# A log-sum-exp without its maximum: range checks and a branch to a safe loop

## The chip, the cores and the metric

The kernel runs on one core of a Trainium2 chip. The metric is the time of one execution on the device, in microseconds (us). The engines are written as the profile writes them: PE is TensorE (PEld its weight loads), DVE is VectorE, ACT is ScalarE, POOL is GpSimd, and SP is SyncE, which here issues nearly all transfers.

## The reference

```
x (8, 2048, 2048) float32, bias (8, 256) float32
B, S, D = x.shape; H = 8; Dh = 256
x_heads = x.reshape(B, S, H, Dh).transpose(0, 2, 1, 3) + bias[None, :, None, :]
x_tiled = np.repeat(x_heads, 2, axis=2)
mx  = x_tiled.max(axis=-1, keepdims=True)
lse = mx.squeeze(-1) + np.log(np.exp(x_tiled - mx).sum(axis=-1))
```

Both inputs are drawn from a standard normal distribution. For each of 8 x 2048 rows and each of 8 heads, one number comes out: the logarithm of the sum of 256 exponentials of x plus bias. Each is written twice, so the output is (8, 8, 4096). The input has 134 MB, the output 1 MB.

## The kernel before

**It takes no maximum.** It sums the exponentials of x + bias as they are and takes the logarithm of the sum. Where a value lies far from zero, such a sum would overflow or vanish; the reference, which subtracts the maximum first, would not.

**Tiles.** The work is cut into 64 tiles of 2 rows on each of 128 partitions (K = 2, 2 MB each), eight tiles to a batch. Eight tiles fit on chip (the buffers xb). SP issues the loads, two tiles at a time up to tile 41 (L158), then one tile or less at a time (L170). A load into a buffer waits for the last reader of the tile that was there eight tiles earlier.

**The work of a bulk tile** (tiles 0 to 53, mode BULK) is split by heads:

- Heads 0 to 2: PE puts the bias into PSUM (L267) and adds x by a product with the identity (L326). ACT takes the exponential. For head 0 it sums on the way (L337, with an accumulator), for heads 1 and 2 it writes the exponentials back (L344).
- Head 3: ACT takes the exponential of x alone (L382), and DVE multiplies it by exp(bias), which lies in PSUM (w_ps, L394).
- Heads 4 to 7: POOL adds the bias in place (L376, a tensor of 128x2048 elements), then ACT takes the exponential (the same L382).
- DVE sums heads 1 to 7 in one reduction (L401, 128x3584).

The sums of batch b go into a tile R[b] of 128 x 128 numbers, those of the last batch into R_last.

**The end of the input** (tiles 54 to 63) runs in other modes, row by row, so that less is left to do when the last bytes land. There DVE multiplies by exp(bias) and sums in one instruction (L417), and POOL folds the last head or two (L433, L441), whose 32 remaining columns DVE sums (L447). ACT's part for PE's heads is L357.

**The output.** Two tiles after a batch has ended, finish(b) transposes its sums on PE (L461) and ACT writes their logarithm, each twice, to res (L471). With the seventh batch done, SP stores seven batches at once (store, L475). For the last batch finish_last does the same at the end: transpose (L482), logarithm (L488), store (L489).

**Order.** The whole kernel stands in a manual schedule: each engine issues its instructions in the order in which the program names them, and semaphores order the engines among each other. After the manual schedule has ended, the closing instructions of the program stand on L623, the line of the surrounding context: the wait for outstanding transfers, a drain of each engine and synchronising events on all of them. Instructions that load the bias and build its factors (L199 to L228) stand before the first tile.

Of the kernel before, what the change touches and what calls it, by code (L numbers as in the profile page):

```python
# [8 lines left out]

F32 = mybir.dt.float32  # L10
BF16 = mybir.dt.bfloat16
ACT = mybir.ActivationFunctionType
ALU = mybir.AluOpType

# [22 lines left out]
SINGLE_F1 = dict(pe=1, acc=1, g0=8, late=False, fold=1)  # L37
TRIPLE = dict(pe=3, acc=3, g0=8, late=False, fold=0)
FOLD = 32

STAGES = [
    (0, (BULK,)),
# [13 lines left out]
def kernel(  # L56
# [6 lines left out]
    nc = tc.nc  # L63
    P = nc.NUM_PARTITIONS
    B, S, D = x.shape
    H, Dh = bias.shape
# [13 lines left out]
    sb = ctx.enter_context(tc.tile_pool(name="sb", bufs=1))  # L80
# [4 lines left out]
    brow = sb.tile([1, D], F32, name="brow")  # L85
    b_rep = sb.tile([P, D - G0], F32, name="b_rep")
    w_sb = sb.tile([P, D - W1], F32, name="w_sb")
    ident = sb.tile([P, P], F32, name="ident")
    ones = sb.tile([1, P], F32, name="ones")
    ones3 = sb.tile([3, P], BF16, name="ones3")  # L90
    b3 = sb.tile([3, CPE], BF16, name="b3")
    bparts = sb.tile([1, 3, CPE], BF16, name="bparts")
    brest = sb.tile([1, 2, CPE], F32, name="brest")

    R = [sb.tile([P, KB, H, NB], F32, name=f"R{b}") for b in range(B - 1)]
    R_last = sb.tile([P, H, NBLK, K], F32, name="R_last")
    res = sb.tile([H * NB, B - 1, P, KB, 2], F32, name="res")
    res_last = sb.tile([P, P, 2], F32, name="res_last")
    xbs = [sb.tile([P, KB, D], F32, name=f"xb{i}") for i in range(NBUF // TB)]
    xts = [xb[:, k : k + K] for xb in xbs for k in range(0, KB, K)]  # L100
    w_ps = pp.tile([P, W2 - W0], F32, name="w_ps")
# [7 lines left out]
    def modes_of(t):  # L109
        return [modes for t0, modes in STAGES if t0 <= t][-1]  # L110

    def pieces(t):

        if len(modes_of(t)) == 1:
            return [(0, K, 0, D)]
        cols = [[(0, D)]] * K if t < T - 1 else LAST_COLS
        return [(k, k + 1, c0, c1) for k in range(K) for c0, c1 in cols[k]]
# [72 lines left out]
    for set_idx, (_name, funcs) in enumerate(get_activation_tables(nc.m.arch).items()):  # L190
        if ACT.Exp in funcs and ACT.Ln in funcs:
            nc.scalar.add_instruction(
                mybir.InstLoadActFuncSet(
                    name=nc.get_next_instruction_name(),
# [23 lines left out]
    def spread(dst, c0, c1):  # L218
        nc.tensor.matmul(  # L219
            dst, lhsT=ones, rhs=brow[:, c0:c1], start=True, stop=True  # L220
        )
# [4 lines left out]
    w_late = w_ps[:, 0 : G0 - W0]  # L226
    spread(w_late, W0, G0)
    nc.scalar.activation(out=w_late, in_=w_late, func=ACT.Exp)  # L228

    def first_factors():  # L230
        spread(one_ps, V0, W0)
        nc.scalar.activation(out=one_ps, in_=one_ps, func=ACT.Exp)

    def other_factors():
        nc.scalar.activation(
            out=w_ps[:, G0 - W0 :], in_=b_rep[:, 0 : W2 - G0], func=ACT.Exp
        )
        nc.scalar.activation(out=w_sb, in_=b_rep[:, W1 - G0 :], func=ACT.Exp)

# [55 lines left out]
    def add_x(m, t, k0, c0, c1, got):  # L295


        heads = []
        for ka, kb, c, w, bank, p in got:
            if not c0 <= c < c1:  # L300
                continue
            mm = nc.tensor.matmul(  # L302
                p,
                lhsT=ident,
                rhs=xts[t % NBUF][:, ka:kb, c : c + w],
                start=False,
                stop=True,
            )
            on_bank(bank, on_x(t, mm, [loads[t, k0, c0]]))
            for i in range(0, (kb - ka) * w, Dh):  # L310
                k, cw = divmod(i, w)
                heads.append((ka + k, (c + cw) // Dh, bank, p[:, i : i + Dh], mm))
        return heads

    def keep_warm():
        for _ in range(NWARM):
            nc.tensor.matmul(  # L317
                tp[:, 0], lhsT=ident, rhs=ident, start=True, stop=True
            )

    def late_heads(m, t, got, sums):
# [13 lines left out]
        def pe_part():  # L335
            for k in range(K):
                act = nc.scalar.activation(  # L337
                    out=xts[t % NBUF][:, k, 0:Dh],
                    in_=got[0][:, k * Dh : (k + 1) * Dh],
                    func=ACT.Exp,  # L340
                    accum_out=sums[:, k, 0:1],
# [87 lines left out]
    def fold(t, k, h0, h1, sums, after):  # L429
# [8 lines left out]
        n = Dh  # L438
        while n > FOLD:
            n //= 2  # L440
# [5 lines left out]
        def add_up():  # L446
            red = nc.vector.tensor_reduce(  # L447
                out=sums[:, k, h0:h1],
                in_=v[:, :, 0:FOLD],
                op=ALU.add,  # L450
# [6 lines left out]
    def finish(b):  # L457

        nr = H * NB
        for k in range(KB):  # L460
            nc.tensor.transpose(  # L461
                out=tp[0:nr, k],
                in_=R[b][:, k].rearrange("p h n -> p (h n)"),
                identity=ident,
            )
        tv = bass.AP(
            tensor=tp.tensor,
            offset=tp.offset,
            ap=[[tp.ap[0][0], nr], [1, P], [P, KB], [0, 2]],
        )  # L470
        nc.scalar.activation(out=res[:, b], in_=tv, func=ACT.Ln)  # L471

    def store():
# [3 lines left out]
            in_=res.rearrange("q b p k r -> q b (p k r)"),  # L477
        )

    def finish_last():  # L480
        last = tp[:, KB - 1]
        nc.tensor.transpose(  # L482
            out=last, in_=R_last.rearrange("p h n k -> p (h n k)"), identity=ident
        )
        tv = bass.AP(
            tensor=last.tensor, offset=last.offset, ap=[last.ap[0], [1, P], [0, 2]]
        )
        nc.scalar.activation(out=res_last, in_=tv, func=ACT.Ln)  # L488
        nc.sync.dma_start(  # L489
            out=out[B - 1].rearrange("h (n r) -> (h n) r", r=2 * P),  # L490
            in_=res_last.rearrange("q p r -> q (p r)"),
        )


    def sums_of(t):

        b, blk = divmod(t, NBLK)
        if b < B - 1:
            return R[b][:, blk % TB * K :, :, blk // TB]
        return R_last[:, :, blk, :].rearrange("p h k -> p k h")  # L500
# [20 lines left out]
    for t in range(T):  # L521
        if t == T_FACTORS:
            other_factors()
        xt = xts[t % NBUF]
        sums = sums_of(t)
        for k0, k1, c0, c1 in pieces(t):
            m = modes_of(t)[k0]
            add = None
            heads = []
            if c0 == 0:  # L530
                bias_here = bias_there
            if m["late"]:
                pe_part = late_heads(m, t, bias_here, sums)
            else:
                heads = add_x(m, t, k0, c0, c1, bias_here)

                def pe_part(t=t, heads=heads, sums=sums):
                    for k, h, bank, p, mm in heads:
                        sum_biased(t, k, h, bank, p, mm, sums)

            if c0 == 0:
                if next_units and not m["late"]:
                    bias_there = put_bias(*next_units.pop(0))
                if t > T_PROMPT and m["g0"] == H:
                    keep_warm()
                if m["g0"] < H:
                    add = g_add(m, t, k0, k1)
                if t < T - 1 or k0 == 0:
                    flush(for_pool)
            if t == T_PROMPT and (k0, c0) == (0, 0):  # L550
                first_factors()
            h0 = max(c0 // Dh, m["pe"])
            h1 = min(c1 // Dh, m["g0"])
            hf = max(h0, min(h1, H - m["fold"]))
            if h0 < h1 and not m["late"]:
                done = exp_inplace(
                    t, xt[:, k0:k1, h0 * Dh : h1 * Dh], loads[t, k0, c0]
                )
                if hf < h1:
                    for_pool.append(fold(t, k0, hf, h1, sums, done))  # L560
            if c0 == 0:
                flush(for_pe)
            if not m["late"]:
                for k in range(k0, k1):
                    for h in range(h0, hf):
                        weigh(
                            t,
                            xt[:, k, h * Dh : (h + 1) * Dh],
                            h,
                            sums[:, k, h : h + 1],  # L570
                            done,
                        )

            def pool_part(t=t, m=m, k0=k0, k1=k1, sums=sums, add=add):
                if add:
                    later(m, t, k0, k1, sums, add)
                if k1 == K:
                    reload(t)

            for_pool.append(pool_part)  # L580
            if m["g0"] < H:
                pe_part()
                if m["late"]:
                    bias_there = put_bias(*next_units.pop(0))
            elif heads:
                for_pe.append(pe_part)

        fb, at = divmod(t - 2, NBLK)
        if fb >= 0 and at == NBLK - 1:
            finish(fb)  # L590
            if fb == B - 2:
                store()
    flush(for_pe)
    flush(for_pool)
    finish_last()

    order.__exit__(None, None, None)


# [28 lines left out]
```

## Time and profile before

| | |
|---|---|
| time, median of 3 runs (lowest to highest) | 325.45 us (325.33 to 326.03) |
| span of the profiled execution, first to last instruction | 323.1 us |
| median of the runs less that span | 2.35 us |
| mean granted TensorE clock | 0.913 |
| last x tile's reduction of the bulk (L401) begins | 276.12 us |
| last sum on DVE (L447) begins | 319.41 us |
| last store issued (L489), median time to landing | 320.52 us, 1.7 us |

The profile comes from one execution and carries no time of its own other than the span; the runs were timed apart from it. The page gives the busy time of each engine, then the span in 40 equal slices with the busy share in tenths, then the queues. The chain of work that ended last is followed back from the last instruction: at each step to whatever released it, or to the instruction before it on its engine. In a list of waits, the columns are the engine and line that waited, what released it, the total in us, the number of times and the longest. In a timeline a row has its start in us, its duration, engine, line, operation, and output and input with their shapes; in square brackets stands how long the engine was idle before, and what ended that. "L12" is line 12 of the kernel.

### The profile page before, as it was taken

The numbers are of one execution on the slowest core, as the hardware profiler recorded it, in microseconds if no ns is written. First come the engines' busy times: TensorE is split into PE (matmuls) and PEld (weight loads), VectorE is DVE, ScalarE is ACT, GpSimd is POOL, SyncE is SP. The second block draws the span as 40 slices with busy tenths as digits, with TensorE's granted clock in tenths as the row PEclk, the third lists the DMA queues.
The fourth block names the chain that finished last, engine by engine and source line by source line (L and its number), as shares of the span: only waits on it lengthen the run. The fifth ranks groups of instructions, "written<-read, shape, count | busy, mean of one in ns | idle before, by whom it ended". The sixth has DMA issues, their size and how long they took to land.

```text
span 323.1 us, 2398 instructions
## 1 busy us (share of the span) xinstructions
PE 270.3 (84%) x691; PEld 102.9 (32%) x691; DVE 283.9 (88%) x306; ACT 265.8 (82%) x426; POOL 287.7 (89%) x120
## 2 busy tenths in 40 slices
PE   5999999889978769977869886888997786599984
PEld 2333333333323223322323322333333232035442
DVE  1037779999999998999899899898999999999995
ACT  1148679889869976988888978889998998899995
POOL 6939998999999999999999999999999999858874
PEclk9979799979979996998997997997999999559998
DMA  8999999999999999999999999999999999999995
GB/s 311 457 402 454 450 400 439 450 402 446 438 414 446 432 418 443 430 422 447 422 426 441 422 434 442 404 426 430 432 422 431 430 428 425 416 422 421 419 401 170
DMA packets 8830, 135.42 MB, mean 419 GB/s; under 512 B 1041, under 2 KB 1425, under 8 KB 2417
## 3 DMA queue, kind: packets, MB, share of 16 engines
q1 hardware_dynamic: 8720, 135.27, 98.6%
q8 instruction: 5, 0.08, 0.1%
q14 instruction: 7, 0.06, 0.0%
q10 hardware_dynamic: 98, 0.01, 0.0%
HBM read 134.23 MB, written 1.05 MB: 419 GB/s over the span
## 4 chain that ended last, share of the span: by engine, by line
DMA 40%; POOL 18%; ACT 17%; PE 14%; DVE 9%; issue 0%; SPq 0%; DVEq 0%
DMA xb<-in_x_dram 40%; POOL xb L376 18%; ACT xb L382 11%; DVE R L401 6%; PE pair L326 5%; PE one_ps L326 3%; PE pair L267 3%; ACT xb L357 2%; PE one_ps L267 2%; DVE xb L417 2%; PE pair L219 1%; ACT xb L337 1%; DVE xb L394 1%; ACT res L471 1%; ACT xb L344 1%; DMA brow<-in_bias_dram 1%
## 5 line engine op out<-in xcount | busy, mean ns | idle before, releaser
L376 POOL TENSOR_TENSOR xb<-xb,b_rep 128x2048 f32<-128x2048 f32 x57 | 257.6, 4539 | 20.7 <-DMA xb<-in_x_dram 20.6
L401 DVE TENSOR_REDUCE R<-xb 128x14 f32<-128x3584 f32 (+1 forms) x56 | 214.5, 3830 | 1.9
L382 ACT ACTIVATE xb<-xb 128x2560 f32<-128x2560 f32 (+5 forms) x77 | 157.1, 2050 | 10.3 <-POOL xb L376 10.1
L326 PE MATMUL pair<-xb,ident 128*128 128x512 f32 x216 | 114.3, 656 | 0.0
L326 PE MATMUL one_ps<-xb,ident 128*128 128x512 f32 x108 | 67.5, 710 | 11.5 <-DMA xb<-in_x_dram 11.5
L344 ACT ACTIVATE xb<-pair 128x1024 f32<-128x1024 f32 x54 | 55.5, 1027 | 23.2 <-PE pair L326 23.0
L326 PEld LDWEIGHTS pair<-xb,ident 128*128 128x128 f32 x216 | 46.2, 214 | 61.3 <-issue 61.3
L394 DVE TENSOR_TENSOR xb<-xb,w_ps 128x512 f32<-128x512 f32 x54 | 36.7, 681 | 26.2 <-ACT xb L382 26.2
L337 ACT ACTIVATE xb<-one_ps 128x256 f32<-128x256 f32 x108 | 40.0, 380 | 6.6 <-PE one_ps L326 6.6
L267 PEld LDWEIGHTS <-ones 3*128 3x128 bf16 (+1 forms) x192 | 16.9, 95 | 80.8 <-issue 71.4
L267 PE MATMUL one_ps<-b,ones 3*128 3x512 bf16 x49 | 18.6, 380 | 25.4 <-ACT xb L337 25.3
L267 PE MATMUL pair<-b,ones 3*128 3x512 bf16 x98 | 29.0, 375 | 0.0
L326 PEld LDWEIGHTS one_ps<-xb,ident 128*128 128x128 f32 x108 | 17.2, 200 | 33.9 <-DMA xb<-in_x_dram 18.0
L302 PE MATMUL pair<-xb,ident 128*128 128x512 f32 (+1 forms) x36 | 21.7, 689 | 5.7 <-DMA xb<-in_x_dram 5.7
L417 DVE CUSTOM_DVE_ANT_0 xb<-xb,w_ps 128x256 f32<-128x256 f32 x61 | 22.4, 418 | 0.0
L337 ACT ACTIVATION_READ_ACCUMULATOR xb<-one_ps 128x1 f32 x108 | 22.3, 207 | 0.0
L441 POOL TENSOR_TENSOR xb<-xb 128x128 f32<-128x128 f32 (+3 forms) x39 | 13.8, 355 | 3.1
L433 POOL TENSOR_TENSOR xb<-xb,w_sb 128x256 f32<-128x256 f32 (+1 forms) x13 | 10.0, 771 | 5.2 <-ACT xb L382 4.5
L317 PE MATMUL tp<-ident 128*128 128x128 f32 x84 | 13.7, 302 | 0.0
L317 PEld LDWEIGHTS tp<-ident 128*128 128x128 f32 x84 | 11.1, 200 | 3.5 <-issue 3.0
L357 ACT ACTIVATE xb<-pair 128x256 f32<-128x256 f32 x33 | 11.9, 364 | 0.0
L417 DVE CUSTOM_DVE_ANT_0 xb<-xb,one_ps 128x256 f32<-128x256 f32 x27 | 10.6, 415 | 0.1
(42 smaller groups left out, 83.4 us busy)
## 6 DMA issues: line engine op xcount, KB each, us to landing
xb<-in_x_dram SPq DMA_DIRECT2D x20, 4096.0 KB, 21.5
xb<-in_x_dram SPq DMA_DIRECT2D x17, 2048.0 KB, 22.7
xb<-in_x_dram SPq DMA_DIRECT2D x12, 1024.0 KB, 22.7
xb<-in_x_dram SPq DMA_DIRECT2D x4, 256.0 KB, 13.2
out_dram<-res SPq DMA_DIRECT2D x1, 896.0 KB, 6.7
xb<-in_x_dram SPq DMA_DIRECT2D x2, 384.0 KB, 15.8
xb<-in_x_dram SPq DMA_DIRECT2D x2, 128.0 KB, 6.3
out_dram<-res_last SPq DMA_DIRECT2D x1, 128.0 KB, 1.7
```

What stands on the lines that cost most here:

```text
L267: nc.tensor.matmul(p, lhsT=lhsT, rhs=each_row(b, h * Dh, Dh, K), start=i == 0, stop=False,)
L302: mm = nc.tensor.matmul(p, lhsT=ident, rhs=xts[t % NBUF][:, ka:kb, c : c + w], start=False, stop=True,)
L317: nc.tensor.matmul(tp[:, 0], lhsT=ident, rhs=ident, start=True, stop=True)
L326: mm = nc.tensor.matmul(p, lhsT=ident, rhs=xts[t % NBUF][:, :, h * Dh : (h + 1) * Dh], start=False, stop=True,)
L337: act = nc.scalar.activation(out=xts[t % NBUF][:, k, 0:Dh], in_=got[0][:, k * Dh : (k + 1) * Dh], func=ACT.Exp, accum_out=sums[:, k, 0:1],)
L344: act = nc.scalar.activation(out=xts[t % NBUF][:, :, Dh : m["pe"] * Dh].rearrange("p k (h j) -> p h k j", j=Dh), in_=got[-1].rearrange("p ...
L357: act = nc.scalar.activation(out=xts[t % NBUF][:, k, h * Dh : (h + 1) * Dh], in_=p, func=ACT.Exp, accum_out=sums[:, k, h : h + 1],)
L376: add = nc.gpsimd.tensor_tensor(out=v, in0=v, in1=each_row(b_rep, c - G0, D - c, k1 - k0), op=ALU.add)
L382: return on_x(t, nc.scalar.activation(out=v, in_=v, func=ACT.Exp), [after])
L394: mul = nc.vector.tensor_tensor(out=f, in0=f, in1=each_row(w_ps, m["pe"] * Dh - W0, n, k1 - k0), op=ALU.mult,)
L401: red = nc.vector.tensor_reduce(out=sums[:, k0:k1, h0:H], in_=v.rearrange("p k (h j) -> p k h j", j=Dh), op=ALU.add, axis=mybir.AxisListTy ...
L417: ttr = nc.vector.tensor_tensor_reduce(out=v, in0=v, in1=w, scale=1.0, scalar=0.0, op0=ALU.mult, op1=ALU.add, accum_out=dst,)
```

## The change

Four things are added, and nothing is taken out.

- At the start DVE finds the largest absolute value of the bias (1x2048 elements) and notes a large number in a tile far if it is over 20.
- Two tiles after each batch, just behind finish(b), and once more at the end for the last batch, how_far(b) treats the bits of the batch's 128 x 128 sums as integers. It subtracts the bits of 1.0 and keeps the largest absolute difference of each partition in a column of far. The bits of a float grow with its exponent, so this measures how many powers of two a sum is away from 1.
- At the end, after finish_last, judge() takes the maximum over the 9 columns of far, transposes the 128 results into one partition on PE, and takes their maximum into an integer, the verdict. Every engine loads the verdict into a register.
- After the manual schedule, a branch compares it with 60 powers of two. If it is larger, all_again() computes everything with the maximum in two nested loops over 8 x 16 blocks of 128 rows; if not, the program goes on to its close.

The diff, without the body of all_again's loop after its load:

```
+BIAS_MAX = 20.0
+ONE_BITS = 127 << 23
+SPAN_BITS = 60 << 23
+TOO_FAR = float(1 << 30)
...
+    far = sb.tile([P, B + 1], F32, name="far")
+    dist = sb.tile([P, P], F32, name="dist")
+    b_far = sb.tile([1, 1], F32, name="b_far")
+    all_far = sb.tile([P, 1], F32, name="all_far")
+    verdict = sb.tile([1, 1], I32, name="verdict")
...
     nc.scalar.activation(out=w_late, in_=w_late, func=ACT.Exp)
+
+    nc.vector.memset(far, 0.0)
+    nc.vector.tensor_reduce(
+        out=b_far, in_=brow, op=ALU.max,
+        axis=mybir.AxisListType.X, apply_absolute_value=True,
+    )
+    nc.vector.tensor_scalar(
+        out=far[0:1, B : B + 1], in0=b_far,
+        scalar1=BIAS_MAX, scalar2=TOO_FAR, op0=ALU.is_gt, op1=ALU.mult,
+    )
...
+    def how_far(b, sums):
+        nc.vector.tensor_scalar(
+            out=dist, in0=sums.bitcast(I32),
+            scalar1=float(ONE_BITS), scalar2=None, op0=ALU.subtract,
+        )
+        nc.vector.tensor_reduce(
+            out=far[:, b : b + 1], in_=dist, op=ALU.max,
+            axis=mybir.AxisListType.X, apply_absolute_value=True,
+        )
+
+    def judge():
+        nc.vector.tensor_reduce(
+            out=all_far, in_=far, op=ALU.max, axis=mybir.AxisListType.X
+        )
+        row = w_ps[0:1, 0:P]
+        nc.tensor.transpose(out=row, in_=all_far, identity=ident)
+        nc.vector.tensor_reduce(
+            out=verdict, in_=row, op=ALU.max, axis=mybir.AxisListType.X
+        )
+        return nc.values_load(
+            verdict, min_val=0, max_val=(1 << 31) - 1,
+            skip_runtime_bounds_check_because="it is only compared, and addresses nothing",
+        )
+
+    def all_again():
+        xt = xbs[0][:, 0]
+        et = xbs[0][:, 1]
+        bt = xbs[1][:, 0]
...
+        nc.sync.dma_start(
+            out=bt, in_=bias.rearrange("h j -> (h j)").unsqueeze(0).to_broadcast([P, D])
+        )
+        rows = x.rearrange("b (n p) d -> b n p d", p=P)
+        outs = out.rearrange("b h (n p r) -> b n p h r", p=P, r=2)
+        with tc.For_i(0, B, 1) as b, tc.For_i(0, S // P, 1) as n:
+            at = (bass.ds(b, 1), bass.ds(n, 1))
+            nc.sync.dma_start(out=xt, in_=rows[at].rearrange("b n p d -> (b n p) d"))
...
             finish(fb)
+            how_far(fb, R[fb].rearrange("p k h n -> p (k h n)"))
             if fb == B - 2:
                 store()
     flush(for_pe)
     flush(for_pool)
     finish_last()
+    how_far(B - 1, R_last.rearrange("p h n k -> p (h n k)"))
+    again = judge() > SPAN_BITS
 
     order.__exit__(None, None, None)
+    with tc.If(again, preferred_fallthrough_block=False):
+        all_again()
```

The part of the loop that is cut adds the bias, takes each head's maximum, its negative, eight exponentials with accumulators, a logarithm, the sum of logarithm and maximum, and one store per round.

More of the change, by code (lines that the diff above doesn't have):

```diff
@@ L11 @@
 BF16 = mybir.dt.bfloat16
+I32 = mybir.dt.int32
 ACT = mybir.ActivationFunctionType
@@ L228 @@
     nc.scalar.activation(out=w_late, in_=w_late, func=ACT.Exp)
+    nc.vector.memset(far, 0.0)
+    nc.vector.tensor_reduce(
+        out=b_far,
+        in_=brow,
+        op=ALU.max,
+        axis=mybir.AxisListType.X,
+        apply_absolute_value=True,
+    )
+    nc.vector.tensor_scalar(
+        out=far[0:1, B : B + 1],
+        in0=b_far,
+        scalar1=BIAS_MAX,
+        scalar2=TOO_FAR,
+        op0=ALU.is_gt,
+        op1=ALU.mult,
+    )
     def first_factors():
@@ L478, in store @@
         )
+    def how_far(b, sums):
+        nc.vector.tensor_scalar(
+            out=dist,
+            in0=sums.bitcast(I32),
+            scalar1=float(ONE_BITS),
+            scalar2=None,
+            op0=ALU.subtract,
+        )
+        nc.vector.tensor_reduce(
+            out=far[:, b : b + 1],
+            in_=dist,
+            op=ALU.max,
+            axis=mybir.AxisListType.X,
+            apply_absolute_value=True,
+        )
[9 more added lines that the diff above has]
+        return nc.values_load(
+            verdict,
+            min_val=0,
+            max_val=(1 << 31) - 1,
+            skip_runtime_bounds_check_because="it is only compared, and addresses nothing",
+        )
@@ new lines, in all_again @@
+    def all_again():
+        xt = xbs[0][:, 0]
+        et = xbs[0][:, 1]
+        bt = xbs[1][:, 0]
+        small = xbs[1][:, 1, 0 : 4 * H].rearrange("p (i h) -> p i h", h=H)
+        mx, neg, total, log = (small[:, i] for i in range(4))
+        both = xbs[1][:, 2, 0 : 2 * H].rearrange("p (h r) -> p h r", r=2)
+        nc.sync.dma_start(
[6 more added lines that the diff above has]
+            nc.sync.dma_start(out=xt, in_=rows[at].rearrange("b n p d -> (b n p) d"))
+            nc.vector.tensor_tensor(out=xt, in0=xt, in1=bt, op=ALU.add)
+            nc.vector.tensor_reduce(
+                out=mx,
+                in_=xt.rearrange("p (h j) -> p h j", j=Dh),
+                op=ALU.max,
+                axis=mybir.AxisListType.X,
+            )
+            nc.vector.tensor_scalar(
+                out=neg, in0=mx, scalar1=-1.0, scalar2=None, op0=ALU.mult
+            )
+            for h in range(H):
+                c = slice(h * Dh, (h + 1) * Dh)
+                nc.scalar.activation(
+                    out=et[:, c],
+                    in_=xt[:, c],
+                    func=ACT.Exp,
+                    bias=neg[:, h : h + 1],
+                    accum_out=total[:, h : h + 1],
+                )
+            nc.scalar.activation(out=log, in_=total, func=ACT.Ln)
+            for r in range(2):
+                nc.vector.tensor_tensor(
+                    out=both[:, :, r], in0=log, in1=mx, op=ALU.add
+                )
+            nc.sync.dma_start(
+                out=outs[at].rearrange("b n p h r -> (b n p) h r"), in_=both
+            )
```

## The prediction

> **What bounds the kernel now.** I read the page first, then the chain of work that ended last, then VectorE's timeline from 20 us to the end, SyncE's own waits, and the groups by form. Busy shares come first.
>
> ```profile
> PE 270.3 (84%) x691; PEld 102.9 (32%) x691; DVE 283.9 (88%) x306; ACT 265.8 (82%) x426; POOL 287.7 (89%) x120
> ...
> DMA  8999999999999999999999999999999999999995
> ...
> HBM read 134.23 MB, written 1.05 MB: 419 GB/s over the span
> ```
>
> The transfers run through all but the first and last of the 40 slices; at 419 GB/s the input alone takes 320 us of a span of 323.1 us. Two MB per tile then take about 5.0 us, against 4.5 us per tile on DVE and on POOL. In the bulk the engines have a little to spare and the DMA queue has none. The end is another matter: the chain leaves the transfers at 282.5 us, runs on ACT to 314.1 us, and then on DVE without a break.
>
> ```profile
> 312.54 1.60 ACT xb L382
> 314.14 0.02 issue
> 314.16 0.42 DVE xb L417
> ...
> 319.50 0.14 DVE R_last L447
> 319.64 0.14 issue
> 319.78 0.32 PE tp L482
> 320.09 0.02 issue
> 320.11 0.38 ACT res_last L488
> ```
>
> After this SP issues the last output at 320.52 us; it lands 1.7 us later, at 322.2 us, and SP waits for it ("SPq L623 <- DMA out_dram<-res_last", 1.2 us). From about 322.4 us to 323.1 us there are only the closing instructions of L623: every engine has two of its synchronising events there, at 322.6 and 323.1 us. So the last 3.5 us are one chain: DVE's last sum, transpose, logarithm, output, close. An engine other than SP has nothing to do in most of it, and this is where the change puts its verdict.
>
> **DVE's idle time** decides what the checks in mid-run cost. These are the last three breaks before the end phase, and the breaks in it:
>
> ```profile
> 206.53 0.69 DVE L394 TENSOR_TENSOR xb<-xb,w_ps 128x512 f32<-128x512 f32 x1 [1.25 <-ACT xb L382]
> 220.97 0.69 DVE L394 TENSOR_TENSOR xb<-xb,w_ps 128x512 f32<-128x512 f32 x1 [0.79 <-ACT xb L382]
> 230.25 0.69 DVE L394 TENSOR_TENSOR xb<-xb,w_ps 128x512 f32<-128x512 f32 x1 [0.15 <-ACT xb L382]
> ...
> 305.38 0.19 DVE L447 TENSOR_REDUCE R_last<-xb 128x1 f32<-128x32 f32 x1 [0.15 <-POOL xb L441]
> 307.46 0.18 DVE L447 TENSOR_REDUCE R_last<-xb 128x1 f32<-128x32 f32 x1 [0.20 <-POOL xb L441]
> 309.55 0.19 DVE L447 TENSOR_REDUCE R_last<-xb 128x1 f32<-128x32 f32 x1 [0.20 <-POOL xb L441]
> 311.63 0.18 DVE L447 TENSOR_REDUCE R_last<-xb 128x1 f32<-128x32 f32 x1 [0.19 <-POOL xb L441]
> ```
>
> In brackets stands how long DVE was idle before. From 230.25 to 305.38 us it never is, and after 311.63 us never again. Whatever is added to DVE after 230 us moves the end, less the 0.15 + 0.20 + 0.20 + 0.19 = 0.74 us of these four waits.
>
> **The change, part by part.** Nothing is removed.
>
> *At the start* DVE gets a memset, a reduction of 1x2048 (2.28 us by the 128x2048 form of L401) and a 1x1 comparison (under 0.2 us, as its 0.17 us memset): 2.6 us. They stand behind the last copy to b_rep, which ends at 8.6 us, and before the first L394, which waits 12.57 us for ACT until 21.15 us. Cost nothing; without that cover, 2.6 us of DVE.
>
> *how_far, seven times in mid-run.* Each is a subtraction over 128x128 and a maximum over 128x128, both on DVE. Reductions of 64 columns took 0.218 us and of 2048 columns 2.284 us, so one of 128 columns takes 0.28 us (1.04 ns a column). The second waits for the first, as L401 does for L394, with a 0.02 us gap; the follower of a reduction starts 0.08 us before its end. Together 0.02 + 0.28 + 0.02 + 0.20 = 0.52 us. The subtraction is not in the trace in this form; 0.22 to 0.28 us bound it. Nobody waits for it. Call b follows the reduction of tile 8b+8; that of tile 40, before call 4, ends at 220.18 us. Calls 0 to 4 are hidden: waits for ACT follow them (0.79 us at 105.30 us, 2.01 at 129.98, 1.00 at 158.17, 0.79 at 182.59, 1.25 at 206.53), and the 0.79 us at 220.97 us covers the last. Call 5 follows the reduction that ends at 257.43 us, call 6 the one that ends at 292.7 us: 1.04 us, less 0.74, so **DVE's last sum comes 0.3 us later**, and the last output with it. Loads wait for DVE ("SPq L158 <- DVE R L401", 172.6 us) and are issued up to 1 us later, but they land 21 to 23 us after their issue while a tile takes 5 us; the queue stays full.
>
> *The verdict.* From DVE's last sum at 319.63 us: subtraction, maximum, a maximum of 9 columns (0.16 us), with gaps, end at 320.41 us. DVE to PE took 0.12 us and PE to its follower 0.36 us at L482: 320.89 us. The last maximum (0.28 us): 321.17 us. With the 0.3 us of above 321.47 us, and with a hop of 0.12 us to each engine, 321.59 us. PE and ACT do this beside the last output; DVE's how_far and the transpose of L482 only read R_last, so neither holds the other.
>
> *The register loads.* Each of five engines reads the verdict from SBUF, side by side, so one counts. No row shows such a load. From below an event on an engine's queue (0.02 to 0.05 us at L623), from above the whole way of a small transfer (the bias row: issued at 0.77, used at 2.82 us, 2.05 us). The nearest is an instruction in which an engine fetches from memory by itself, ACT's table load at 1.28 us; I take that: 322.87 us. Comparison and branch are a few queue instructions, 0.1 us: 322.97 us. SP would close at 322.4 + 0.3 = 322.70 us, so 0.27 us stick out. The Trainium skill, "DMA: Bandwidth & Descriptors", section "Latency and other measured facts", gives a floor of about 600 ns for a tensor load; with that the verdict would be in by 322.3 us, all under the output, and the sum 0.3 us smaller.
>
> *The branch itself.* Its arm contains transfers and two loops, and what follows must find the engines and semaphores in one state whichever way was taken. That may cost nothing, or what the kernel's own close costs: from 322.40 to 323.14 us, 0.74 us with two synchronising events per engine. I take the upper end, since this is the one row of the same kind: 0.74 us.
>
> **Sum**: 0.30 + 0.27 + 0.74 = 1.31 us. The span of 323.1 us plus what lies around it is the median of the runs (325.45 - 323.1 = 2.35 us, taken as unchanged): 325.45 + 1.31 = **326.8 us**. By the bounds (load 0.05 to 2.05 us, branch 0 to 0.74 us) this case goes up to 325.45 + 0.30 + 1.04 + 0.74 = 327.5 us; below 326.1 us it turns into the first rival.
>
> **Rivals.**
>
> *The cover holds (not slower).* If load plus branch take less than 322.70 - 321.59 = 1.1 us and the arms need no synchronising, everything but the 0.3 us lies beside the last output: 325.75 us. It decides at that 1.1 us and at an evening-out below 0.35 us. For it: four engines are idle for 2.6 us there. Against it: the only fetch by an engine itself takes 1.28 us.
>
> *The next code is not there.* The page has 12 instruction packets (q8 and q14) for code loaded while the engines run. If the untaken way ends in a jump over the loop's code to a place that is not loaded, one engine waits for a packet, and all wait for it: up to 2.05 us by the bias row, 328.8 us. Against it: the arm that goes straight on is asked for, and the loop is short.
>
> *DVE's subtraction waits for POOL.* It is the first DVE instruction here that reads SBUF alone and writes SBUF, and POOL's adds of 4.54 us stand back to back around it. No row of the bulk shows such a pair. From below nothing. From above a call waits for the add under way, on average half of it, 2.27 us: for seven calls 6 x (2.27 + 0.52) + 0.52 = 17.3 us, less all of DVE's idle time from 99 us to the end, 7.7 + 0.74 us: DVE 8.8 us late, 335.3 us with the rest. If DVE's phase stays as it is, only call 5 counts: POOL's add ends at 258.2 us, 0.8 us after the call, 327.6 us. Against it: the one DVE instruction with two inputs in SBUF starts at 319.07 us, its usual 0.35 us after its forerunner, while POOL works until 319.17 us.
> The Trainium skill, "SBUF — State Buffer", section "Who interferes with whom", speaks for it and against this change: a tensor_scalar can take a port pair shared with GpSimd as an exclusive lock, and the second comer is blocked for a whole instruction. By that rule the sum would be the 335 us and not the 326.8 us; I give the row at 319.07 us more weight, though it is short.
>
> *The branch is taken.* Then 128 rounds each load 1 MB and cannot overlap: more than 300 us more. Sums of 256 exponentials of numbers of order one are thousands, far from the bounds at 2 to the 60 either way. Under 1 in 100.
>
> **How the numbers follow.** Forecast 0.50, cover holds 0.17, code 0.13, POOL 0.18, anything else 0.02. A measurement can tell about 0.2% from no change, 0.65 us, so "same" reaches from 324.8 to 326.1 us. It takes the cover's 0.17 and 0.03 of the forecast's lower edge: 0.20. Faster has no mechanism, 0.02; slower 0.78. The range of 8 in 10 runs from 325.7 to 332 us: it leaves out the lower end of the cover (0.05), the upper two thirds of the POOL case (0.12) and the rest (0.02).
>
> **What would show it.** On DVE: pairs of 0.22 to 0.28 us after tiles 48 and 57, with DVE's last sum 0.3 us later against the start; a break of more than 1 us before a subtraction is the POOL case. At the end: the verdict 1.8 us behind the last sum; then the time from it to the first closing event, 1.4 us if the load is 1.28 us. An extra synchronising round on all engines after the output shows the branch's cost; instruction packets in the last 3 us, with idle engines and no barrier, show the code case. A later landing of the inputs, or POOL waiting longer for loads, would prove me wrong on the full queue.

## The result and the profile after

| | before | after |
|---|---|---|
| time, median (lowest to highest) | 325.64 us (325.33 to 326.03, 4 runs) | 335.88 us (335.59 to 355.5, 4 runs) |
| ratio of the times, 95% interval | | 1.0306 [1.0289, 1.0322] |
| span of the profiled execution | 323.1 us | 334.0 us |
| time of that execution | not taken | 335.89 us |
| DVE's last sum (L447 before, L477 after) ends | 319.63 us | 329.79 us |
| from there to the end of the span | 3.5 us | 4.2 us |

Three runs of the changed kernel took 335.59 to 335.89 us; a fourth took 355.5 us and is left out of the ratio. The change costs 10 us, 3%. The span is 10.9 us longer: 10.16 us of that are there when DVE writes its last sum, 0.7 us come behind it.

First the page of the changed kernel: the busy times, the transfers and the chain that ended last.

```profile
PE 271.2 (81%) x692; PEld 103.6 (31%) x692; DVE 305.5 (91%) x327; ACT 263.6 (79%) x426; POOL 287.6 (86%) x120
...
DMA  8999999999999999999999999999999999999920
...
DVE 85%; PE 12%; ACT 1%; issue 1%; DMA 0%; DVEq 0%
```

Before, the transfers held 40% of the chain, now 0%, and DVE alone holds 85%. DVE has 21.6 us more work by the records, although the change names only about 7 us of it. POOL has as much as before.

The groups of DVE by form show where the rest is (columns: line, engine, operation, output and input, count, total us, mean ns, idle before):

```profile
L512 DVE TENSOR_SCALAR dist<-R 128x128 f32<-128x128 int32 x7 | 18.5, 2640 | 0.0
L519 DVE TENSOR_REDUCE far<-dist 128x1 f32<-128x128 f32 x8 | 2.3, 286 | 0.3
...
L512 DVE TENSOR_SCALAR dist<-R_last 128x128 f32<-128x128 int32 x1 | 0.2, 227 | 0.1
```

It is one instruction, how_far's subtraction. Seven times in mid-run it took 2.64 us on average; the eighth time, on the last batch, the same instruction on the same size took 0.23 us. The maximum behind it takes 0.29 us everywhere. What differs for the eighth is that POOL is done by then. The timeline of DVE and POOL about call 5 shows the rest:

```profile
259.57 3.89 DVE L431 TENSOR_REDUCE R<-xb 128x14 f32<-128x3584 f32 x1
263.32 4.54 POOL L406 TENSOR_TENSOR xb<-xb,b_rep 128x2048 f32<-128x2048 f32 x1 [0.36 <-DMA xb<-in_x_dram]
263.37 4.57 DVE L512 TENSOR_SCALAR dist<-R 128x128 f32<-128x128 int32 x1
267.98 0.29 DVE L519 TENSOR_REDUCE far<-dist 128x1 f32<-128x128 f32 x1
268.23 4.55 POOL L406 TENSOR_TENSOR xb<-xb,b_rep 128x2048 f32<-128x2048 f32 x1 [0.36 <-DMA xb<-in_x_dram]
```

POOL's add begins 0.05 us before the subtraction and ends at 267.86 us; the subtraction ends at 267.94 us. It is the same at each of the seven calls: the subtraction ends 0.08 to 0.09 us behind the end of one of POOL's instructions (72.23 behind 72.14, 111.10 behind 111.01, and so on). Note how it is recorded: the bracket with DVE's idle time is missing. The blocked instruction counts as running; only its duration, against 0.23 us, tells of the wait.

What DVE loses, it first takes out of its own idle time. Before, it waited ten times for ACT between 99 and 231 us, 7.7 us in total; after, it never does there, and the 0.74 us of the end phase are gone too.

### The profile page after: what moved, and what is told of

Its sections match the earlier page's. It is cut to its first block, busy times and chain, and to the rows that moved or that the text cites. A ratio compares the mean times of both kernels' runs of the same rounds, so it can differ in the third digit from the quotient of the medians.

```text
span 334.0 us, 2450 instructions
## 1 busy us (share of the span) xinstructions
PE 271.2 (81%) x692; PEld 103.6 (31%) x692; DVE 305.5 (91%) x327; ACT 263.6 (79%) x426; POOL 287.6 (86%) x120
## 4 chain that ended last, share of the span: by engine, by line
DVE 85%; PE 12%; ACT 1%; issue 1%; DMA 0%; DVEq 0%
DVE R L431 60%; DVE xb L424 9%; DVE xb L447 9%; DVE dist L512 5%; PE pair L356 4%; PE one_ps L356 2%; PE pair L297 2%; PE one_ps L297 1%; PE pair L232 1%; DVE far L519 1%; ACT xb L412 1%; DVE R_last L431 1%; DMA brow<-in_bias_dram 0%; DVE R_last L477 0%; ACT xb L374 0%
## 5 line engine op out<-in xcount | busy, mean ns | idle before, releaser
L501 ACT ACTIVATE res<-tp 32x1024 f32<-32x1024 f32 x7 | 7.1, 1014 | 21.4 <-PE tp L491 21.4
L332 PE MATMUL pair<-xb,ident 128*128 128x512 f32 (+1 forms) x36 | 21.0, 670 | 2.9 <-DMA xb<-in_x_dram 2.9
L367 ACT ACTIVATION_READ_ACCUMULATOR xb<-one_ps 128x1 f32 x108 | 23.1, 214 | 0.0
L447 DVE CUSTOM_DVE_ANT_0 xb<-xb,w_ps 128x256 f32<-128x256 f32 x61 | 22.4, 418 | 0.0
L491 PE MATMUL tp<-ident,R 128*32 128x128 f32 x28 | 6.4, 324 | 18.8 <-DVE R L431 18.8
L512 DVE TENSOR_SCALAR dist<-R 128x128 f32<-128x128 int32 x7 | 18.5, 2640 | 0.0
L347 PE MATMUL tp<-ident 128*128 128x128 f32 x84 | 14.4, 313 | 0.0
```

Source lines behind the costliest of these rows:

```text
L332: mm = nc.tensor.matmul(p, lhsT=ident, rhs=xts[t % NBUF][:, ka:kb, c : c + w], start=False, stop=True,)
L347: nc.tensor.matmul(tp[:, 0], lhsT=ident, rhs=ident, start=True, stop=True)
L367: act = nc.scalar.activation(out=xts[t % NBUF][:, k, 0:Dh], in_=got[0][:, k * Dh : (k + 1) * Dh], func=ACT.Exp, accum_out=sums[:, k, 0:1],)
L447: ttr = nc.vector.tensor_tensor_reduce(out=v, in0=v, in1=w, scale=1.0, scalar=0.0, op0=ALU.mult, op1=ALU.add, accum_out=dst,)
L512: nc.vector.tensor_scalar(out=dist, in0=sums.bitcast(I32), scalar1=float(ONE_BITS), scalar2=None, op0=ALU.subtract,)
```

## The experiments

Four theories stood against each other. **L**: the subtraction reads and writes SBUF and can't run while POOL's add does; it waits for the add's end. **W**: the subtraction over integers is slow in itself. **D**: it waits for those who write or read R. A fourth, that the branch and the program behind it cost the time, needs no POOL at all. The kernel before ran beside each experiment: medians of 325.30, 325.46, 325.51 and 325.85 us on the four occasions.

| run | median us | ratio to before [95%] |
|---|---|---|
| e1_psum | 326.41 | 1.0038 [1.0024, 1.0053] |
| e2_reduce | 325.81 | 1.0013 [1.0003, 1.0023] |
| e3_tail | 326.09 | 1.0019 [1.0010, 1.0028] |
| e4_mid | 332.87 | 1.0200 [1.0142, 1.0258] |
| e5_split | 355.65 | 1.0921 [1.0903, 1.0939] |
| e6_f32 | 335.65 | 1.0307 [1.0286, 1.0327] |
| e7_two | 334.97 | 1.0286 [1.0265, 1.0307] |
| e8_before_split | 325.86 | 1.0011 [1.0001, 1.0020] |
| e9_no_if | 325.35 | 1.0002 [0.9989, 1.0014] |
| e10_no_verdict | 325.30 | 0.9993 [0.9983, 1.0004] |
| e11_split_psum | 326.51 | 1.0038 [1.0024, 1.0053] |
| e12_again | 335.64 | 1.0278 [1.0228, 1.0327] |
| e13_no5 | 330.99 | 1.0161 [1.0144, 1.0178] |
| e14_only5 | 330.37 | 1.0143 [1.0126, 1.0160] |

### e1_psum: only the place of the result is another

```
     def how_far(b, sums):
+        to = tp[:, 0] if b < B - 2 else dist
         nc.vector.tensor_scalar(
-            out=dist,
+            out=to,
...
-            in_=dist,
+            in_=to,
```

> The six subtractions of batches 0 to 5 write to PSUM (the bank of tp) and not to SBUF; those of batches 6 and 7 stay. Theory L (a subtraction that reads and writes SBUF can't run beside POOL's add and waits for its end): each of the six takes about 0.3 us, DVE's last sum comes within 1 us of the kernel before, time 326.6 us (326.1 to 327.3). Rival W (the subtraction over 128x128 integers is slow in itself) and rival D (it waits for the readers or writers of R): the six still take 1.7 to 4.6 us, time 335 to 337 us.

DVE's groups of this run:

```profile
L520 DVE TENSOR_REDUCE far<-tp 128x1 f32<-128x128 f32 x6 | 1.7, 291 | 0.2
L513 DVE TENSOR_SCALAR tp<-R 128x128 f32<-128x128 int32 x6 | 1.7, 284 | 0.0
```

All six took 0.28 us, beside adds of POOL that were running. Input, type, size, place in the program and everything they wait for are as before. 9.5 of the 10.2 us are gone. D and W fall here; what is left needs the output of the subtraction to lie in SBUF. (The seventh, of batch 6, still wrote to SBUF; it ended 0.1 us behind one of POOL's short folds and took 0.22 us.)

### e7_two and e6_f32: neither the size nor the type

```
         nc.vector.tensor_scalar(              # e7_two
-            out=dist,
-            in0=sums.bitcast(I32),
+            out=dist[:, 0:2],
+            in0=sums.bitcast(I32)[:, 0:2],
...

         nc.vector.tensor_scalar(              # e6_f32
             out=dist,
-            in0=sums.bitcast(I32),
-            scalar1=float(ONE_BITS),
+            in0=sums,
+            scalar1=1.0,
```

> Subtraction and maximum of each check take 2 of the 128 columns; the other 126 sums of a partition are not tested. Theory L: the size doesn't matter, each of the six in mid-run still ends about 0.1 us after one of POOL's adds has ended and takes up to 4.5 us; time 332 to 336 us. Rival W (work of the subtraction): under 0.2 us each, time 326.2 us.

> The subtraction takes the sums as float32 (1.0 is subtracted) and not their bits as integers, so that the test of the range is another one. Theory L: the type doesn't matter, the six still end with POOL's adds, time 332 to 336 us. A rival in which reading integers is what is slow: 0.3 us each, time 326.6 us.

With two columns in place of 128 the six took 4.54, 2.65, 2.87, 2.66, 1.72 and 4.37 us, with floats 3.66, 2.53, 2.52, 2.61, 1.79 and 4.30 us. Call 5 of the run with two columns:

```profile
263.42 4.37 DVE L512 TENSOR_SCALAR dist<-R 128x2 f32<-128x2 int32 x1
```

Two numbers per partition, and 4.37 us. Again each ended 0.02 to 0.1 us behind one of POOL's adds. This is pure waiting.

### e3_tail and e4_mid: the two ends of the change apart

e3_tail leaves out the call of how_far in the loop over the tiles; e4_mid leaves out everything behind finish_last, the branch with its loop among it.

> The seven checks in mid-run are left out, so that only the last batch and the bias are tested; verdict, loads and branch stay. Theory L: what is left is the end alone, 0.5 to 0.8 us in the profile, time 326.2 us (325.8 to 326.6). If the new end or the longer program costs more than the profile shows, over 327 us.

> The checks in mid-run stay, the last batch's check, the verdict, the loads, the branch and the loop are left out. Theory L: DVE is as late as in the changed kernel, only the end is short again: 335.2 us (334.6 to 335.6). If the branch or the loaded program slowed the whole run, under 330 us.

The end alone costs 0.19%, 0.6 us by the ratio. The checks in mid-run alone cost 2% (1.4 to 2.6%), with a wide spread: 330.24, 330.81, 334.93 and 335.07 us. I had expected the upper pair only. The branch is not the cause; but the price of the checks is not one number either.

### e2_reduce: the same test without the subtraction

```
     def how_far(b, sums):
-        nc.vector.tensor_scalar(out=dist, in0=sums.bitcast(I32), ...)
-        nc.vector.tensor_reduce(out=far[:, b : b + 1], in_=dist, op=ALU.max, ...)
+        for c, op in ((b, ALU.max), (B + b, ALU.min)):
+            nc.vector.tensor_reduce(
+                out=far[:, c : c + 1], in_=sums, op=op, axis=mybir.AxisListType.X
+            )
```

The sums are positive, so their largest and smallest value per partition say as much as the largest distance. far has 17 columns then, one of them for the bias, and judge() subtracts the bits of 1.0 from these 17 at the end.

> Every check in mid-run becomes two reductions of the sums themselves, a maximum and a minimum; the one subtraction, over 17 columns, stands at the end, where POOL is done. All bounds are still tested. Theory L: a reduction doesn't meet POOL, each takes 0.28 us, time 326.5 us (326.0 to 327.2). Rival D: the first reduction of a call reads R just as the subtraction did and waits as long: 335 to 336 us. Rival W allows 326.5 us too.

```profile
L512 DVE TENSOR_REDUCE far<-R 128x1 f32<-128x128 f32 x14 | 3.3, 278 | 0.0
```

Fourteen reductions of 0.28 us, none of them held up, though twelve lie wholly within an add that POOL was running; DVE's last sum ends at 319.73 us, 0.1 us after that of the kernel before. They read R where the subtraction read it, which is a second refutation of D. They also read SBUF and write SBUF (far), as the subtraction does: so theory L, as it stands above, is too wide. It holds for this form of instruction, the subtraction by a constant, and not for reductions. The kernel tests all that the changed one tests, and it costs 0.13% instead of 3%.

### e5_split, e8_before_split, e11_split_psum: shorter adds, and a surprise

```
-        v = xts[t % NBUF][:, k0:k1, c:D]
-        add = nc.gpsimd.tensor_tensor(
-            out=v, in0=v, in1=each_row(b_rep, c - G0, D - c, k1 - k0), op=ALU.add
-        )
+        for k in range(k0, k1):
+            v = xts[t % NBUF][:, k : k + 1, c:D]
+            add = nc.gpsimd.tensor_tensor(
+                out=v, in0=v, in1=each_row(b_rep, c - G0, D - c, 1), op=ALU.add
+            )
```

e5_split has this edit on the changed kernel, e8_before_split on the kernel before, e11_split_psum on e1_psum.

> The changed kernel, with each of POOL's adds over 128x2048 cut into two over 128x1024. Theory L, with the lock held for one instruction: no subtraction lasts longer than half an add, 2.3 us, on average 1.1 us; DVE late by 6 x (1.1 + 0.5) + 0.8 - 8.4 = 2 us at most, time 326.5 to 329 us. If a subtraction has to wait until POOL pauses, it lasts up to 4.5 us and longer as before, and the time stays at 333 to 336 us.

> The kernel before with the same cut of POOL's adds, for comparison. Each add may cost 0.05 to 0.1 us more, POOL has 0.3 us per tile to spare: 325.3 to 326 us. If the cut alone costs more, the run with the subtractions has to be read against it.

> Adds cut in two, as in the run that took 355.65 us, with the subtractions of batches 0 to 5 written to PSUM. If the 28 us that one subtraction took there is the same lock, held on from one add to the next, it vanishes: each of the six 0.28 us, 326.5 to 327.5 us. If the cut adds bring something else, over 340 us.

The cut alone costs 0.1%. With the subtractions it took 355.65 us, 20 us more than the uncut kernel, where I had expected 7 to 9 us less. The first five calls took 1.56, 0.22, 0.41, 1.16 and 1.88 us, as expected under half an add. The sixth did not. DVE's timeline, then POOL's:

```profile
255.66 3.89 DVE L435 TENSOR_REDUCE R<-xb 128x14 f32<-128x3584 f32 x1
259.47 28.49 DVE L516 TENSOR_SCALAR dist<-R 128x128 f32<-128x128 int32 x1
287.99 0.29 DVE L523 TENSOR_REDUCE far<-dist 128x1 f32<-128x128 f32 x1
```

```profile
257.81 30.06 POOL L408 TENSOR_TENSOR xb<-xb,b_rep 128x1024 f32<-128x1024 f32 x13
299.75 0.73 POOL L467 TENSOR_TENSOR xb<-xb,w_sb 128x256 f32<-128x256 f32 x1 [11.88 <-ACT xb L416]
```

The first of these is one subtraction of 28.49 us. POOL's row merges 13 adds, one behind the other without a pause. The subtraction let twelve of them end and got in 0.09 us behind the last, when POOL had run out of work (the bracket: 11.88 us idle). DVE frees the buffers, so SP issued no loads from 260.0 to 293.2 us ("SPq L183 <- DVE R L435", longest 32.8 us), and the transfers themselves came to a halt. This is the full price of the lock: it isn't bounded by one add. With the output in PSUM (e11_split_psum) the six took 0.28 us each, in the same program with the same cut adds: 326.51 us.

The 355.5 us run among the first four of the changed kernel has the time and the span of these (353.7 us against 353.8 to 353.9 us). A stall of the same kind is likely there; it is not shown, since no trace of that run was kept.

### e12_again, e13_no5, e14_only5: what the price depends on

e12_again is the changed kernel without an edit. The two others are:

```
-            how_far(fb, R[fb].rearrange("p k h n -> p (k h n)"))
+            if fb != 5:                     # e13_no5;  e14_only5: if fb == 5:
+                how_far(fb, R[fb].rearrange("p k h n -> p (k h n)"))
```

> The changed kernel again, unchanged, for the spread of its times. If a subtraction gets in between two adds that stand back to back only by chance, then besides 335.9 us there are times near 355 us, as one of its first four runs had; if that one was an outside disturbance, all are within 1 us of 335.9 us.

> The changed kernel without the check of batch 5, the one whose subtraction took 4.57 us because it came 0.05 us after an add had begun. If this one call decides between the times near 335.8 us and those near 330.8 us, all times are now near 330.8 us (330 to 331.5). If the calls before it weigh as much, the time stays above 333 us or falls below 329 us.

> Of the seven checks in mid-run only that of batch 5. DVE then comes to it at about 257.5 us, in a row of adds without a pause, 0.8 us before one of them ends. If it gets in at that end: a subtraction of 0.8 to 1 us, time 326.3 to 327 us. If it has to wait until POOL pauses: 5 us or more, 330 us and above.

e12_again gave 335.60 to 335.80 us five times and 330.78 us once, and none of the six is near 355 us. e13_no5 gave 330.94 to 331.58 us five times and 326.41 us once, and that one is in the profile:

```profile
67.07 0.69 DVE L512 TENSOR_SCALAR dist<-R 128x128 f32<-128x128 int32 x1
105.61 1.03 DVE L512 TENSOR_SCALAR dist<-R 128x128 f32<-128x128 int32 x1
143.56 1.98 DVE L512 TENSOR_SCALAR dist<-R 128x128 f32<-128x128 int32 x1
183.29 1.40 DVE L512 TENSOR_SCALAR dist<-R 128x128 f32<-128x128 int32 x1
221.33 1.53 DVE L512 TENSOR_SCALAR dist<-R 128x128 f32<-128x128 int32 x1
```

All five were held up, by 0.5 to 1.8 us, so little that DVE's idle time paid for most of it: DVE's last sum ends at 320.56 us, 0.9 us after that of the kernel before. In the 335.89 us run of the changed kernel the same five took 4.06, 2.51, 2.54, 2.54 and 1.76 us. The times lie in steps, 326.4 and 331 us for e13_no5, 330.8 and 335.7 us for the changed kernel, about one add of 4.54 us apart. The two traces suggest why: call 0 came just before an add ended at 67.68 us in the one and just after an add had ended at 67.66 us in the other, where it waited for the next end at 72.14 us. That this sets the step in the other runs is not shown, since no trace of a 331 us run of either program was kept. Going by the times, call 5 is worth a step, as I had thought, but it is not the only one.

e14_only5 fits neither of its two expectations. DVE, then the two adds that the subtraction met:

```profile
257.84 5.33 DVE L512 TENSOR_SCALAR dist<-R 128x128 f32<-128x128 int32 x1
263.20 0.29 DVE L519 TENSOR_REDUCE far<-dist 128x1 f32<-128x128 f32 x1
```

```profile
254.07 4.54 POOL L406 TENSOR_TENSOR xb<-xb,b_rep 128x2048 f32<-128x2048 f32 x1
...
258.58 4.51 POOL L406 TENSOR_TENSOR xb<-xb,b_rep 128x2048 f32<-128x2048 f32 x1
...
263.10 4.55 POOL L406 TENSOR_TENSOR xb<-xb,b_rep 128x2048 f32<-128x2048 f32 x1
```

The subtraction was ready 0.77 us before the first add ended, at 258.61 us, and did not get in. It got in at the second end, at 263.09 us, although the third add followed without a pause. One call out of seven costs 4.6 us by DVE's last sum (324.28 us against 319.63 us), 1.4% of the kernel. Twelve ends were passed over in one run and one in another, each time by the call of batch 5; every other subtraction in the traces that met an add got in at the next end. What lets it in at one end and not at another stays open.

### e9_no_if and e10_no_verdict: the end, taken apart

e9_no_if is e2_reduce without the branch and the loop; e10_no_verdict also lacks the verdict and the register loads.

> The version with reductions in mid-run, with verdict and register loads but without the branch and its loop, so nothing is recomputed. If the branch and what follows it cost the 0.5 us at the end (SP goes through its waits only after the branch, where before it had them behind it when the output landed), the time from DVE's last sum to the end falls from 4.1 us to about 3.6 us, 325.4 us. If the register loads cost it, it stays at 4.1 us and 325.8 us.

> The version with reductions in mid-run, without verdict, loads, branch and loop: the seventeen small DVE instructions alone. If they are free, as the trace of the reductions suggests (DVE's last sum 0.1 us later), 325.4 us, within 0.1% of the kernel before; by the count of DVE's idle time 0.3 us more, 325.6 us.

The small DVE instructions are free, and so are verdict and loads: both runs are within what can be told from the kernel before. Between 325.81 us with the branch and 325.35 us without lie 0.46 us, 0.11% by the ratios, whose intervals overlap, so the times alone do not settle it. The profiles say the same: from DVE's last sum to the first closing drain of SP it is 2.75 us without the branch (322.47 less 319.72) and 3.27 us with it (323.00 less 319.73).

## Why the prediction was wrong

**The step that failed** is the price of how_far: "Together 0.02 + 0.28 + 0.02 + 0.20 = 0.52 us." The subtraction was bounded at 0.22 to 0.28 us; it took 0.49 to 4.57 us. The bounds came from rows in which DVE works beside POOL undisturbed (reductions), and I called them bounds for an instruction that the trace did not show. Alone the subtraction takes 0.23 us and into PSUM 0.28 us, so the size was right and the neighbour was missing. The prediction also misread its rows where it called the subtraction the first DVE instruction that reads SBUF alone and writes SBUF. The reductions of L401 do so too, 54 times in the bulk:

```profile
L401 DVE TENSOR_REDUCE R<-xb 128x14 f32<-128x3584 f32 x54 | 209.9, 3887 | 1.9
```

What was new was the form of the instruction, and no row of the kernel before has it beside POOL.

**The choice behind it** was that between a rule and a row. The Trainium skill, "SBUF — State Buffer", section "Who interferes with whom", gave the mechanism, and the sum by it was 335.3 us against 335.88 us measured. I set against it one instruction at 319.07 us, which has two inputs in SBUF and overlapped the last 0.10 us of POOL's last fold:

```profile
318.85 0.32 POOL L441 TENSOR_TENSOR xb<-xb 128x64 f32<-128x64 f32 x1
319.07 0.42 DVE L417 CUSTOM_DVE_ANT_0 xb<-xb,w_sb 128x256 f32<-128x256 f32 x1
```

That row could not carry it: another instruction, in another form, and only the last tenth of a microsecond of POOL's work. What these runs show agrees with the page in that the two exclude each other (4.57 us beside an add, 0.23 us alone, 0.28 us with the output in PSUM) and goes beyond it: a DVE instruction waited through twelve GpSimd instructions, not one.

**The POOL rival's price** (8.8 us late on DVE, 10.16 us measured) came out near, by the average of half an add per call, less DVE's idle time. That is partly luck: the average hides that the price comes in steps (330.78 us in another run of the same kernel), and that there is no upper end of one add. Its cheaper variant, with call 5 alone at 0.8 us and 327.6 us in all, failed: in e14_only5 that call took 5.33 us and the run 330.37 us. The chance of the rival, 0.18, was far too low.

**The cover by the full queue** held: the transfers stay at 9 tenths and more up to the last two slices although DVE is 10 us late. It ended only in the run with the 28 us stall.

**The start** was right. The reduction of the bias took 2.26 us from 8.00 us on, and DVE then still waited 9.12 us for ACT.

**The verdict** was right: 1.54 us were predicted from DVE's last sum to the verdict, and the last maximum ends at 331.40 us, 1.61 us after 329.79 us.

**The end** was over-priced in both terms. These are the waits of SP behind the last store, in the changed kernel:

```profile
SPq L596 <- ACT res_last L595: 16.2, 1, 16.2
SPq L735 <- PEq L735: 0.6, 2, 0.4
SPq L536 <- DVE verdict L533: 0.2, 1, 0.2
```

SP waited 1.2 us for the output before; that row is gone, since the output has landed when SP looks. The register loads took 0.665 to 0.684 us on each of the five engines (331.42 to 332.12 us) and not the 1.28 us of ACT's table load. The 600 ns of the Trainium skill ("DMA: Bandwidth & Descriptors", section "Latency and other measured facts"), which the prediction also gave, were nearer, but they are no floor here: in e2_reduce the five loads took 0.48 to 0.54 us. The loads lie under the output, which lands 1.7 us after its issue at 330.83 us, so the first half of the cover rival was right. The branch brings no round of synchronising events: comparisons of 0.04 to 0.17 us and a few events on L708, from 332.16 to 332.54 us. Then SP goes through eight waits of the close one by one, about 0.06 us each, until 333.21 us; the kernel before had four, two of them behind it when the output landed. That is 0.5 us in place of 0.27 + 0.74 us. The rest of the 0.7 us shows beside e13_no5, which has the same end and 4.06 us in place of 4.21 us behind the last sum: the transpose of judge() took 0.37 us here and 0.27 us there, SP's register load 0.67 us and 0.62 us.

**The code rival** cost nothing, although its sign was there in part: with the branch a packet of q14, the queue of instructions, stands just behind it (333.39 to 333.90 us; in e2_reduce 323.19 to 323.59 us), and without it (e9_no_if) none does. No engine waited for it: from SP's first closing drain to the end of the span it is 0.79 us in e2_reduce and in e9_no_if alike. **The branch was not taken.** What lies around the span was taken as unchanged at 2.35 us. That figure set the median of the runs against the span of another execution; where both stand for one execution, the kernel before has 2.1 to 2.2 us. All kernels with range checks have 1.7 to 2.0 us (335.89 less 334.0 for the changed one). I have no cause for this difference.

**The chain** runs from the transfers at 282.5 us through one of POOL's adds (4.55 us) and only then on ACT, which the prediction left out; no term rests on it.

## What to carry to other kernels

Before adding an instruction to a busy engine, ask which resource of its neighbour it takes, and not only how long it runs: a 0.23 us subtraction, called seven times in mid-run, cost 10 us because it waited for GpSimd's adds as long as its output lay in SBUF. A rule that names a mechanism should be given up only for a row that shows that very pair. Reductions straight from the data did the same test for 0.1%, and an output in PSUM for six of the eight checks for 0.4%.

## What the runs showed of the hardware that was not expected

- The DVE subtraction that was blocked by GpSimd shows no idle time: the whole wait is in its duration (28.49 us for a 0.23 us subtraction).
- The wait is not bounded by one GpSimd instruction. Adds let the subtraction in at the next end, or after one or twelve ends passed over; shorter adds (2.3 us in place of 4.5 us) made it worse here, not better, with 355.65 us in place of 335.64 us, by one call out of six.
- A register load from SBUF took 0.67 us in the changed kernel and 0.48 to 0.69 us over all traces. Five engines that did it at once differed by at most 0.07 us within a run; no run has one engine alone.
- A reduction on DVE of the same 128x128 sums, from SBUF to SBUF, ran in 0.28 us within POOL's adds: of the two forms only the subtraction was held up.
